# One decoder layer on one core: the end reads x1 and y ahead of the last two down weights and splits the last sum between DVE and PE; the start fills two experts' operands early

## The chip, the cores and the metric

The kernel runs on one core of a Trainium2 chip. The number that counts is the device time of one execution in microseconds (us). The engines are PE (matrix multiply), DVE (vector), ACT (scalar), POOL (GpSimd) and SP, which here only issues transfers; every engine works through its own instructions in the order in which they are written. ACT and POOL issue some transfers too. The transfers of all three run on the core's 16 DMA engines.

## The reference, cut to what matters

One layer: a mixer (differential attention and latent attention), an output projection, a LayerNorm that gives x1, a router that picks 4 of 32 experts for each of 512 tokens, the experts, and a second LayerNorm.

```python
x = layer_norm(DN_ALPHA * x + mixed, ln1_g[l], ln1_b[l])          # x1
logits = (xt @ w_router + b_router); top_logit, top_idx = lax.top_k(logits, TOP_K)
gates = jax.nn.softmax(top_logit, axis=-1)
# each expert, for the tokens that chose it:
h = xb @ w_gate_up[e] + b_gate_up[e]
act = (up + 1.0) * (gate * jax.nn.sigmoid(gate * SWIGLU_ALPHA))   # gate and up are clamped halves of h
y = act @ w_down[e] + b_down[e]                                    # weighted by the token's gate and summed
x = layer_norm(DN_ALPHA * x + y, ln2_g[l], ln2_b[l])
```

All is float32. The experts' weights are 32 x (8 MB gate and up + 4 MB down); each is read once, in pieces of 1 MB.

## The kernel before

**Tiles.** The 512 tokens are four tiles of 128. Attention goes through (tile, head) units in an order written out by hand (`ORDER`, `PLAN`); after each tile come its output projection, LayerNorm, router logits, and `ranks`, which counts the tile's tokens for each expert. The last two tiles go through `last_two`.

**Weight stream.** `Stream` holds a list of pieces in the order of use: w_in, w_o, then for expert b its 8 gate-and-up pieces, with the 4 down pieces of expert b-1 behind them; the last are gate-and-up of expert 31, down of 30, down of 31. `ahead()` (the issue is L165) sends the next pieces on SP while there are free 1 MB rooms (`raw`, 11 in the ring and a twelfth later) and while `hold` and `limit` allow. SP works in order, so a transfer that waits holds up all that stand behind it. Here "piece" means such a 1 MB read.

**Experts.** For b = 0 to 31: `gu(b)` (gate and up, 8 steps, one piece each, with small tasks of `between(k)` ahead of each step), `swiglu(b)`, and then `down(b - 1)` (4 pieces). Experts 0 and 1 here are the two least used ones after two tiles (`pick_first`), and have 32 token slots each; 30 and 31 have 64. A gather by POOL brings an expert's token rows from x1 in DRAM (`x1d`) into `xg`; PE transposes them into the operand xT. A scatter by POOL writes the result to `yd` in DRAM. Experts 30 and 31 are kept on the chip instead (`y_keep`) and added by matmuls (`tail_kept`); their scatters only serve a later loop that does not run for these inputs.

**Start of the experts.** At the end of the second `ranks` the kernel picks experts 0 and 1, sends the first weight pieces, and for expert 0 alone computes slot columns (`columns`, `prep_tile`), indices (`prep2`, a small matmul at L1356) and the gather (L1378). `last_two` adds the rows of the last two tiles to expert 0's operand by matmuls with a one-hot matrix (`first_col`, `first_more`, L1346, in the PSUM tile `xT0`). The biases are read on ACT's queue (`bias_early`, L1283) ahead of the last tile's norm. Expert 1's operand is prepared inside `gu(0)` with a gather of its own.

**End.** z holds x1 of the four tiles, ys the four expert rows of each token: eight 1 MB reads of `yd`, two for a tile. z is read by `tail_setup` in `gu(30)` (L1664). In `gu(31)` the first six reads of `yd` (L1726) go out when the stream has nothing more to send but down of 31; `tail_gb` and `tail_gates` (L1678 and others) are small tasks between the steps. After `gu(31)`: `tail_sum` of tiles 0 to 2 on DVE (L1731, four instructions of 128x1024 for a tile), `down(30)`, `tail_add` (identity matmul of z into PSUM at L1749, the kept expert 30 at L1739, then the last two reads of `yd` and tile 3's sum on DVE), `down(31)`, and `tail`: expert 31 added, statistics of each tile (L1775 on DVE, square root on POOL), and `finish`: for tiles 0 to 2 ACT normalises, DVE multiplies (L1788), POOL adds (L1789); tile 3 is all DVE; SP writes out (L1795).

## Time and profile before

| | us |
|---|---|
| three runs | 1361.19, 1361.88, 1357.73 (median 1361.19) |
| the profiled execution | 1357.27 |
| its span, first to last instruction | 1355.4 |
| PE, DVE, ACT, POOL busy | 1239.3, 708.5, 534.1, 154.7 |

The page cuts the span into 40 slices and gives for each the busy share of every engine, the granted TensorE clock and the rate of the transfers. The timeline lists an engine's instructions in order of time, equal neighbours merged, and in brackets how long the engine had been idle before and what released it. The windows give busy time, clock and transfer rate of any stretch.

### The profile page before, as it was taken

Reading aid. Unit: us, or ns where it says so; the run is one execution under the profiler, and the core shown is the slowest. Engines: PE = TensorE matmul, PEld = TensorE weight load, DVE = VectorE, ACT = ScalarE, POOL = GpSimd, SP = SyncE. Lnnn points to the kernel's source line nnn. Section 1 sums busy time; section 2 is a strip of 40 time slices with the busy share of each in tenths; the row PEclk is TensorE's granted clock in tenths of the full one; section 3 lists DMA queues with packets and bytes.
Section 4 is the critical chain, followed back from the end, with each engine's and each line's share of the span. In section 5 each row is a group of like instructions: output and inputs, shape, how many; then the busy total and the mean of one; then the engine's idle time right before and its main releaser. Section 6 shows DMA issues by size and latency. Waiting matters only on the chain.

```text
span 1355.4 us, 17704 instructions
## 1 busy us (share of the span) xinstructions
PE 1239.3 (91%) x6376; PEld 784.1 (58%) x6376; DVE 708.5 (52%) x1279; ACT 534.1 (39%) x795; POOL 154.7 (11%) x177
## 2 busy tenths in 40 slices
PE   6989698787999999899999999998999998999892
PEld 5768597773368853354444675464657754765330
DVE  4554655455279931433533685264657745753055
ACT  3442543311167730323413564254455534643111
POOL 2232200010100001001100100000111000000004
PEclk9999799797999999999999999999999999999797
DMA  9201620469999999999999999999999999999981
GB/s 327 98 1 62 231 100 32 177 225 409 416 419 420 418 420 420 420 415 419 419 372 419 419 418 419 419 420 419 419 418 418 417 417 409 415 419 415 395 363 73
DMA packets 76411, 465.28 MB, mean 343 GB/s; under 512 B 10176, under 2 KB 11376, under 8 KB 26144
## 3 DMA queue, kind: packets, MB, share of 16 engines
q1 hardware_dynamic: 65680, 434.89, 78.5%
q0 software_dynamic: 7584, 18.47, 3.7%
q10 hardware_dynamic: 3056, 10.75, 2.1%
q8 instruction: 52, 0.85, 0.3%
q14 instruction: 39, 0.32, 0.1%
HBM read 445.33 MB, written 25.30 MB: 347 GB/s over the span
## 4 chain that ended last, share of the span: by engine, by line
PE 52%; DMA 31%; DVE 7%; ACT 3%; POOL 2%; issue 1%; ACTq 0%; SPq 0%; POOLq 0%; DVEq 0%
DMA raw<-in_w_gate_up_dram 19%; PE acc L1450 13%; DMA raw<-in_w_down_dram 8%; PE acc L266 8%; PE acc L267 8%; PE acc L268 8%; DVE wlo L260 2%; DMA yr<-yd 1%; DMA raw<-yd 1%; PE ip L266 1%; PE ip L268 1%; PE ip L267 1%; PE po L689 1%; PE zp L268 1%; PE zp L266 1%
## 5 line engine op out<-in xcount | busy, mean ns | idle before, releaser
L260 DVE TENSOR_TENSOR wlo<-raw,whi 128x1024 fp32r<-128x1024 f32 (+3 forms) x331 | 393.7, 1238 | 108.8 <-ACT whi L259 105.6
L259 ACT CAST whi<-raw 128x1024 fp32r<-128x1024 f32 (+3 forms) x331 | 335.1, 1063 | 139.7 <-DMA raw<-in_w_gate_up_dram 48.3
L1450 PE MATMUL acc<-raw,xTs 128*64 128x512 f32 (+1 forms) x1344 | 286.4, 621 | 11.5 <-DMA raw<-in_w_gate_up_dram 10.1
L266 PE MATMUL acc<-whi,xTh 128*128 128x512 f32 x416 | 167.8, 403 | 1.8 <-ACT whi L259 1.6
L267 PE MATMUL acc<-wlo,xTh 128*128 128x512 f32 x416 | 164.0, 394 | 3.1 <-DVE wlo L260 3.0
L1450 PEld LDWEIGHTS acc<-raw,xTs 128*64 128x64 f32 (+1 forms) x1344 | 75.7, 133 | 154.9 <-issue 126.9
L268 PE MATMUL acc<-whi,xTl 128*128 128x512 f32 x416 | 163.7, 393 | 0.0
L1450 PE MATMUL acc<-raw,aTs 128*64 128x512 f32 (+1 forms) x736 | 122.6, 526 | 1.9 <-DMA raw<-in_w_down_dram 1.9
L1561 POOL DMA_INDIRECT yd<-y,idx x34 | 46.1, 1356 | 651.7 <-ACT y L1550 472.2
L1500 DVE TENSOR_SCALAR u<-acc 128x512 f32<-128x512 f32 (+1 forms) x47 | 31.1, 661 | 166.1 <-ACT s L1499 166.1
L266 PEld LDWEIGHTS acc<-whi,xTh 128*128 128x128 f32 x416 | 78.2, 188 | 32.8 <-ACT whi L259 8.9
L1499 ACT ACTIVATE s<-acc 128x512 f32<-128x512 f32 (+1 forms) x47 | 26.9, 573 | 166.0 <-PE acc L1455 91.4
L267 PEld LDWEIGHTS acc<-wlo,xTh 128*128 128x128 f32 x416 | 78.1, 188 | 22.4 <-DVE wlo L260 6.2
L268 PEld LDWEIGHTS acc<-whi,xTl 128*128 128x128 f32 x416 | 78.2, 188 | 17.5
L267 PE MATMUL acc<-wlo,aTh 128*128 128x512 f32 x208 | 81.9, 394 | 4.3 <-DVE wlo L260 4.3
L1450 PEld LDWEIGHTS acc<-raw,aTs 128*64 128x64 f32 (+1 forms) x736 | 41.2, 129 | 73.5 <-issue 61.4
L266 PE MATMUL acc<-whi,aTh 128*128 128x512 f32 x208 | 82.4, 396 | 0.5 <-ACT whi L259 0.5
L268 PE MATMUL acc<-whi,aTl 128*128 128x512 f32 x208 | 81.8, 393 | 0.0
L1378 POOL DMA_INDIRECT xg<-x1d,idx x34 | 41.0, 1205 | 307.9 <-issue 168.6
L1550 ACT COPY y<-acc 128x512 f32<-128x512 f32 (+2 forms) x32 | 23.2, 725 | 120.8 <-PE acc L268 72.5
L1358 DVE TENSOR_REDUCE lv<-tp 128x2 f32<-128x4 f32 x35 | 5.6, 159 | 113.6 <-PE tp L1356 113.5
L1406 DVE SCALAR_TENSOR_TENSOR aTl<-tp,aTh 128x512 fp32r<-128x512 f32 x26 | 16.7, 685 | 81.7 <-ACT aTh L1402 81.6
(343 smaller groups left out, 1557.8 us busy)
## 6 DMA issues: line engine op xcount, KB each, us to landing
raw<-in_w_gate_up_dram SPq DMA_DIRECT2D x256, 1024.0 KB, 20.4
raw<-in_w_down_dram SPq DMA_DIRECT2D x128, 1024.0 KB, 21.0
yd<-xg ACTq DMA_DIRECT2D x4, 2048.0 KB
raw<-in_w_in_dram SPq DMA_DIRECT2D x6, 1024.0 KB, 13.7
raw<-yd SPq DMA_DIRECT2D x5, 1024.0 KB, 19.9
raw<-in_w_o_dram SPq DMA_DIRECT2D x4, 1024.0 KB, 5.0
yr<-yd SPq DMA_DIRECT2D x3, 1024.0 KB, 19.9
raw<-in_x_dram SPq DMA_DIRECT2D x4, 512.0 KB, 8.9
```

The source lines that it names most:

```text
L259: nc.scalar.copy(hi[:, js], t[:, js])
L260: nc.vector.tensor_tensor(lo[:, js], t[:, js], hi[:, js].bitcast(F32), op=ALU.subtract)
L266: nc.tensor.matmul(out, l[0], r[0], start=start, stop=False)
L267: nc.tensor.matmul(out, l[0], r[1], start=False, stop=False)
L268: nc.tensor.matmul(out, l[1], r[0], start=False, stop=stop)
L1378: nc.gpsimd.indirect_dma_start(out=B["xg"], out_offset=None, in_=self.rows(self.x1d, n), in_offset=bass.IndirectOffsetOnAxis(ap=B["idx"][: ...
L1406: nc.vector.scalar_tensor_tensor(lo, v, scale, hi.bitcast(F32), op0=ALU.mult, op1=ALU.subtract)
L1450: self.nc.tensor.matmul(o[n * i:n * i + n], lT, r, start=start, stop=stop)
L1499: nc.scalar.activation(s, ps[:, :w], AF.Silu, scale=SW)
L1500: nc.vector.tensor_scalar(u, ps[:, w:2 * w], LIM + 1.0, 1.0 - LIM, op0=ALU.min, op1=ALU.max)
L1550: nc.scalar.copy(y, B["d"])
L1561: self.nc.gpsimd.indirect_dma_start(out=self.rows(self.yd, n), out_offset=bass.IndirectOffsetOnAxis(ap=B["idx"][:, 1:2], axis=0), in_=y, i ...
```

## The change

At the end, x1 of all tiles and the six reads of `yd` for tiles 0 to 2 are issued together at the start of `gu(31)`, behind its last gate-and-up piece and ahead of the down pieces of experts 30 and 31 (`hold` now stops the stream 8 pieces before its end). z is no longer scaled by ACT; gates divided by ALPHA are used in the sums (`ga`) and ALPHA comes in through a diagonal matrix (`diag`). `tail_sum` of tiles 0 to 2 moves into `tail_add`. Tile 3 is split by columns: its second half is summed by PE, with `diag` holding one gate per token (L1830), its first half by DVE, after the statistics of tiles 0 to 2. The scatter of expert 31 moves behind those statistics.

At the start, experts 0 and 1 are both prepared from the first two tiles, in the next two steps of the plan after the second `ranks`; `first_more` adds the last two tiles' rows to both in one matmul of 2 x 32 columns; both operands go to free columns of `xg[0]`. Expert 1's late gather and transposes in `gu(0)` go away, and its slot columns for the scatter move to steps 6 and 7 and into `gu(1)`. The bias reads go to POOL's queue behind the last tile's logits. Five 512-column matmuls whose result nobody reads (`warm`) are added behind the last tile's logits and ranks.

```diff
-            def first_col(q):
-                B = self.blk[0, 0]
-                nc.vector.scalar_tensor_tensor(self.scr[:, :E], self.rk1[:, q], 1.0, self.at0, ...
+            def first_cols(q):
+                mf = w.tile([P, 2, 32], F32, name="mf1", tag="e", bufs=10)
+                for b in range(2):
...
-                    B = self.blk[0, 0] = {}
-                    self.at0 = self.columns(B, 0, w)
-                    for t in ranked:
-                        self.prep_tile((0, 0), t)
-                    self.prep2((0, 0), ranked)
-                    self.gather((0, 0))
+                    self.one = []
+                    early_cols(0)
+                    soon.extend([0, 1])
...
+            def early_rows(b):
+                self.prep2((b, 0), ranked[:2])
+                self.gather((b, 0))
+                if b == 0:
+                    early_cols(1)
+
+            def warm(n):
+                ps = po.tile([P, 512], F32, name="po", tag="po")
+                for j in range(n):
+                    nc.tensor.matmul(ps, self.ident, lng[:, :512], start=j == 0, stop=j == n - 1)
...
-                self.bias_early(nc.scalar)
...
+                self.bias_early(nc.gpsimd)
                 logits2(q)
+                warm(3)
                 self.rank(q)
...
+                warm(2)
+                mq = first_cols(q)
...
                 convert()
+                if soon:
+                    early_rows(soon.pop(0))
...
         self.z = [r[:, j * D:(j + 1) * D] for r in rooms[1:] for j in range(2)]
-        for t in range(NT):
-            nc.sync.dma_start(self.z[t], self.x1d[t * P:(t + 1) * P])
+        self.st.hold = len(self.st.src) - KD
...
         if k == 0:
-            self.ys, self.limit = [], 0
-        if k == 4:
-            self.limit = self.nslots
+            for t in range(NT):
+                nc.sync.dma_start(self.z[t], self.x1d[t * P:(t + 1) * P])
+            self.ys = []
+            self.tail_y(2 * NT - 2)
+            st.hold = len(st.src)
             st.ahead()
-        if k < 4:
-            self.tail_y(2 * NT - 2)
...
-        if k > 3:
-            nc.scalar.mul(self.z[k - 4], self.z[k - 4], ALPHA)
...
     def tail_add(self):
...
         for t in range(NT - 1):
-            self.tail_first(t)
+            self.tail_sum(t, D)
+            for n in range(2):
+                self.tail_first(t, n)
+        self.tail_first(NT - 1, 1)
         self.tail_y(2 * NT)
         self.scatter(B["y"], B, 2)
-        self.tail_sum(NT - 1)
...
-        self.tail_first(NT - 1)
-        self.tail_kept(NT - 1, b, True)
+        self.tail_kept(q, 1, b, False)
+        for k in range(TOPK):
+            nc.tensor.matmul(self.zp[q][1], self.diag[:, k],
+                             self.ys[2 * q + k // 2][:, k % 2 * D + 512:(k % 2 + 1) * D], start=False,
+                             stop=k == TOPK - 1)
+        for t in range(q):
+            stats(t)
+        self.tail_sum(q, 512)
+        self.tail_first(q, 0)
+        self.tail_kept(q, 0, b, True)
         self.scatter(B["y"], B, 2)
-        stats(0)
-        stats(1)
-        for t in range(NT):
-            if t + 2 < NT:
-                stats(t + 2)
+        finish(0)
+        stats(q)
+        for t in range(1, NT):
             finish(t)
```

How the change moves instructions is seen at three places. First SP's transfers at the end of the stream (`raw` from in_w_down are weight pieces, the first four of expert 30, the next four of 31; `yr` and `raw` from yd are the reads of expert rows). Before:

```order
L165 DMA raw_9458<-in_w_gate_up_dram 128x2048
L1664 DMA yr<-x1d 128x1024 x4
...
L165 DMA raw_9494<-in_w_gate_up_dram 128x2048
...
L165 DMA raw_9514<-in_w_down_dram 128x2048
...
L165 DMA raw_9532<-in_w_down_dram 128x2048
L1726 DMA yr<-yd 128x2048 x3
L1726 DMA raw_9550<-yd 128x2048
...
L165 DMA raw_9606<-in_w_down_dram 128x2048
...
L1726 DMA raw_9721<-yd 128x2048
```

After:

```order
L165 DMA raw_9517<-in_w_gate_up_dram 128x2048
L1726 DMA yr<-x1d 128x1024 x4
L1751 DMA yr<-yd 128x2048 x3
L1751 DMA raw_9562<-yd 128x2048
...
L165 DMA raw_9568<-in_w_down_dram 128x2048
...
L165 DMA raw_9620<-in_w_down_dram 128x2048
...
L165 DMA raw_9641<-in_w_down_dram 128x2048
...
L1751 DMA raw_9754<-yd 128x2048
```

The x1 reads now stand behind the last gate-and-up piece, and six reads of `yd` stand ahead of the down pieces of expert 30 instead of behind them.

Second, PE between `down(30)` and the end (`zp` of the four tiles lies in the PSUM tiles `acc` and `tp`; L1450 and L1469 are the expert matmuls, L1428 and L1447 the transposes of expert 31's activations). Before:

```order
L1428 MATMUL tp<-cst,u 128x128 x4
L1749 MATMUL acc<-yr,cst 128x512 x2
L1739 MATMUL acc<-y,mg 128x512 x2
...
L1455 MATMUL acc<-biasr,selw 128x512
L1450 MATMUL acc<-raw_9606,aTs 64x512 x4
...
L1739 MATMUL tp<-y,mg 128x512 x2
L1749 MATMUL acc<-yr,cst 128x512 x2
L1739 MATMUL acc<-y,mg 128x512 x4
```

After:

```order
L1447 MATMUL tp<-cst,u 128x128 x4
L1766 MATMUL acc<-yr,diag 128x512
L1762 MATMUL acc<-y,mg 128x512
...
L1474 MATMUL acc<-biasr,selw 128x512
L1469 MATMUL acc<-raw_9641,aTs 64x512 x4
...
L1830 MATMUL acc<-raw_9754,diag 128x512 x2
L1830 MATMUL acc<-raw_9756,diag 128x512 x2
L1766 MATMUL acc<-yr,diag 128x512
L1762 MATMUL acc<-y,mg 128x512 x2
```

Between the two down products stand seven half tiles instead of six, and behind the second one four matmuls for half of tile 3's sum are new.

Third, PE at the second `ranks` (L1211 and L1228 end `pick_first`; L1356 and L1375 are `prep2` for the early gathers; `po` and `sc` belong to attention). Before:

```order
L1211 MATMUL tp<-sel,oneb 128x32
L1356 LDWEIGHTS m
L1356 MATMUL tp<-orh,m 128x4
...
L689 MATMUL po<-raw_804,pT 128x128
...
L645 MATMUL sc<-raw_474,raw_480 128x128
```

After:

```order
L1228 MATMUL tp<-sel,oneb 128x32
L689 MATMUL po<-raw_804,pT 128x128
...
L645 MATMUL sc<-raw_474,raw_480 128x128
...
L1375 LDWEIGHTS m
L1375 MATMUL tp<-orh,m 128x4
...
L676 MATMUL tp<-cst,e 128x128 x2
```

The first `prep2` moved behind a step of attention; the second one, for expert 1, comes a step later still.

## Rows read from the trace of the kernel before

**Rows 1.** The page: transfer rate (GB/s) in 40 slices of the span

```profile
GB/s 327 98 1 62 231 100 32 177 225 409 416 419 420 418 420 420 420 415 419 419 372 419 419 418 419 419 420 419 419 418 418 417 417 409 415 419 415 395 363 73
```

**Rows 2.** Windows: stretch, length, busy PE, PEld, DVE, ACT, POOL (count), PEclk, DMA share, GB/s

```profile
250.00:258.00 8.00, 2.06 (x17) 1.89 (x15) 5.81 (x32) 1.73 (x6) 0.41 (x1) 0.70 0.23 72
276.00:288.00 12.00, 11.81 (x79) 10.42 (x77) 5.64 (x10) 2.78 (x5) 1.69 (x2) 1.00 0.01 1
310.00:340.00 30.00, 24.33 (x164) 9.80 (x163) 16.88 (x84) 4.73 (x10) 1.59 (x2) 0.75 1.01 420
```

**Rows 3.** Timeline of SP's issues, the last 120 us

```profile
1250.55 7.79 SPq L1664 DMA_DIRECT2D yr<-x1d  x4
1260.62 8.18 SPq L165 DMA_DIRECT2D raw<-in_w_gate_up_dram  x4
1269.69 4.15 SPq L165 DMA_DIRECT2D raw<-in_w_down_dram  x4
1275.97 5.24 SPq L1726 DMA_DIRECT2D yr<-yd  x3
1290.97 7.80 SPq L165 DMA_DIRECT2D raw<-in_w_down_dram  x4
1300.88 2.83 SPq L1726 DMA_DIRECT2D raw<-yd  x2
```

**Rows 4.** Transfer issues from 1230 us on: KB each, median us to landing

```profile
raw<-in_w_down_dram SPq DMA_DIRECT2D x11, 1024.0 KB, 19.8
```

**Rows 5.** Timeline of PE, from gu(31) to the end

```profile
1270.26 1.15 PE L1678 MATMUL tp<-gb,cst 16*128 16x128 f32 x8
1275.93 3.68 PE L1450 MATMUL acc<-raw,xTs 128*64 128x512 f32 x8 [4.52 <-DMA raw<-in_w_gate_up_dram]
1294.98 7.09 PE L1450 MATMUL acc<-raw,aTs 128*64 128x512 f32 x32
1301.99 0.75 PE L1428 MATMUL tp<-cst,u 128*128 128x128 f32 x4
1312.47 1.98 PE L1749 MATMUL tp<-yr,cst 128*128 128x512 f32 x4 [0.41 <-DVE yr L1731]
1315.45 0.51 PE L1455 MATMUL acc<-biasr,selw 128*128 128x512 f32 x1
1315.88 7.09 PE L1450 MATMUL acc<-raw,aTs 128*64 128x512 f32 x32
1323.65 1.99 PE L1739 MATMUL acc<-y,mg 64*128 64x512 f32 x8 [0.69 <-ACT y L1558]
```

**Rows 6.** Timeline of DVE at the end

```profile
1296.86 7.76 DVE L1731 SCALAR_TENSOR_TENSOR yr<-yr,gates 128x1024 f32<-128x1024 f32 x6
1304.65 7.76 DVE L1731 SCALAR_TENSOR_TENSOR yr<-raw,gates,yr 128x1024 f32<-128x1024 f32 x6
1320.76 5.25 DVE L1731 SCALAR_TENSOR_TENSOR yr<-raw,gates,yr 128x1024 f32<-128x1024 f32 x4 [8.35 <-DMA raw<-yd]
1325.93 1.29 DVE L1775 BATCH_NORM_STATS2 bs<-acc 128x6 f32<-128x512 f32 x2
```

**Rows 7.** Timeline of POOL at the end

```profile
1336.24 0.51 POOL L283 TENSOR_SCALAR rs_t<-mv 128x1 f32<-128x1 f32 x1
1338.03 5.83 POOL L1789 TENSOR_TENSOR yr<-yr 128x512 f32<-128x512 f32 x4
```

**Rows 8.** Windows of PE alone: stretch, length, busy (count), PEclk, DMA share, GB/s

```profile
1274.00:1290.00 16.00, 14.06 (x40) 0.50 1.01 420
1308.00:1311.00 3.00, 3.00 (x6) 0.50 1.03 426
```

**Rows 9.** Timeline at the second ranks and up to the third tile's x1 store, by engine

```profile
256.37 0.35 PE L1356 MATMUL tp<-orh,m 128*128 128x4 bf16 x2 [5.94 <-DVE m L1315]
287.44 0.33 SPq L788 DMA_DIRECT2D x1d<-z  x1
303.92 1.07 ACT L783 COPY x1T<-tp 128x512 f32<-128x512 f32 x2 [9.64 <-DMA braw<-in_b_gate_up_dram]
```

More of the change, by code (lines that the diff above doesn't have):

```diff
@@ L860, in attention @@
             tasks = (mix_all, lambda q: out_proj(q, 0), lambda q: out_proj(q, 1), norm, logits, logits2, ranks)
-            todo, late = [], []
+            todo, late, soon = [], [], []
             def flush():
@@ L922, in attention @@
             assert ended == len(started) and [f for f, _ in todo[:2]] == [logits2, ranks] and len(todo) == 9
+            assert not soon
             last_two(*done[-2:])
@@ L1063, in moe @@
         self.oh = mp.tile([P, 2, E], F32, name="oh")
-        xT = mp.tile([P, 2, 4, 32], F32, name="xTs", tag="xTh")
-        nc.scalar.copy(xT, self.xT0[:, :256].rearrange("p (k h s) -> p k h s", k=2, h=4))
+        for b in range(2):
+            xT = self.xg[0][:, 512 + 256 * b:768 + 256 * b].rearrange("p (k h s) -> p k h s", k=2, h=4)
+            nc.scalar.copy(xT, self.xT0[:, b * 256:(b + 1) * 256].rearrange("p (k h s) -> p k h s", k=2, h=4))
+            self.blk[b, 0]["xT"] = xT
         self.rest()
@@ L1076, in first_between @@
         def first_between(k):
-            if k == 0:
-                self.columns(self.blk.setdefault((1, 0), {}), 1, mp)
-                self.prep((1, 0))
-            elif k == 2:
-                self.prep2((1, 0))
-                self.gather((1, 0))
-            elif k == 3:
+            if k == 2:
                 for b in range(2):
@@ L1153, in moe @@
                     self.load_xT(u)
-            if b == KEPT[1]:
-                for t in range(NT - 1):
-                    self.tail_sum(t)
             if b > 0:
@@ L1334, in prep_sel, with first_rows @@
                 self.nc.vector.tensor_scalar(B["sel"][j], self.oneb, oh[j], None, op0=ALU.mult)
-    def first_rows(self, rows):
-        for k in range(2):
-            self.nc.tensor.matmul(self.xT0[:, k * P:(k + 1) * P], rows[:, k * P:(k + 1) * P], self.ident,
-                                  start=k == 0, stop=False)
+    def first_rows(self):
+        for b in range(2):
+            for k in range(2):
+                c = b * 256 + k * P
+                self.nc.tensor.matmul(self.xT0[:, c:c + P], self.xg[b][:, k * P:(k + 1) * P], self.ident,
+                                      start=c == 0, stop=False)
     def first_more(self, rows, mf, last):
@@ L1345, in first_more @@
             c = k % 2 * P + k // 2 * 32
-            self.nc.tensor.matmul(self.xT0[:, c:c + 32], rows[:, k * P:(k + 1) * P], mf, start=False,
-                                  stop=last and k == KD - 1)
+            o = self.xT0.rearrange("p (b n) -> p b n", b=2)[:, :, c:c + 32]
+            self.nc.tensor.matmul(o, rows[:, k * P:(k + 1) * P], mf, start=False, stop=last and k == KD - 1)
     def prep2(self, u, tiles=range(NT)):
@@ L1726, in tail_y, with tail_sum @@
             self.nc.sync.dma_start(self.ys[-1], yv[t, :, j * 2 * D:(j + 1) * 2 * D])
-    def tail_sum(self, t):
+    def tail_sum(self, t, w):
         for k in range(TOPK):
-            self.nc.vector.scalar_tensor_tensor(self.z[t], self.ys[2 * t + k // 2][:, k % 2 * D:(k % 2 + 1) * D],
-                                                self.gates[:, t, k:k + 1], self.z[t], op0=ALU.mult, op1=ALU.add)
-    def tail_kept(self, t, b, stop):
-        B = self.blk[b, 0]
-        for n, o in enumerate(self.zp[t]):
-            ns = slice(64 * n, 64 * n + 64)
-            self.nc.tensor.matmul(o, B["mg"][ns, t * P:(t + 1) * P], B["y"][ns], start=False, stop=stop)
@@ L1741, in tail_first @@
-    def tail_first(self, t):
-        if t == 2:
-            self.zp[t] = [self.tp() for _ in range(2)]
-        else:
-            v = self.acc()
-            self.zp[t] = [v[:, n * 512:(n + 1) * 512] for n in range(2)]
-        for n, o in enumerate(self.zp[t]):
-            self.nc.tensor.matmul(o, self.ident, self.z[t][:, n * 512:(n + 1) * 512], start=True, stop=False)
-        self.tail_kept(t, KEPT[0], False)
+            self.nc.vector.scalar_tensor_tensor(self.z[t][:, :w], self.ys[2 * t + k // 2][:, k % 2 * D:k % 2 * D + w],
+                                                self.ga[:, t, k:k + 1], self.z[t][:, :w], op0=ALU.mult, op1=ALU.add)
```

59 lines of the change are left out of this document (43 added, 16 removed).

## The prediction

> **What bounds the kernel now.** I read the page's row of transfer rates first [rows 1]: from the tenth slice of the span to the thirty-ninth the transfers run at about 420 GB/s with small dents. One window inside shows what that means: at 310 to 340 us the 16 DMA engines are busy to 1.01 of the time [rows 2] while PE works 24.33 of 30 us. So between the start of the stream and its end PE follows the transfers, and what the change gains or loses there on PE, ACT or DVE is covered. Only two stretches can move the end: what comes before the stream is saturated, and what comes after its bytes run out.
>
> At the start, the transfers stand almost still at 276 to 288 us (1 GB/s, PE busy 11.81 of 12) [rows 2]. SP stands in order behind the store of the third tile's x1, which it issues at 287.44 [rows 9]. This hole ends when PE has brought the third tile that far; the saturated stream begins there.
>
> At the end, the order on SP decides [rows 3]. The last two reads of yd are issued at 1300.88 and 1303.7. A 1 MB read lands 19.8 us after its issue [rows 4], so the second one lands at about 1323.5. DVE waited 8.35 us for the reads, has tile 3's sum at 1320.76 to 1326.0, and goes on with the statistics [rows 6]. PE ends down(31) at 1315.88 + 7.09 = 1322.97 [rows 5], so that two chains arrive nearly together. From there it is epilogue: POOL's four adds end at 1338.03 + 5.83 = 1343.86 [rows 7], 20.9 us behind down(31), and the store and the program's end follow.
>
> All sums below stand on the profiled execution: 1357.27 us, of which its span is 1355.4 and 1.87 lies around it. The median of the three runs is 1361.19, 3.9 above it.
>
> **Tail: the order of the transfers.** The reads of yd go out at 1275.97 for the first and 1300.88 for the seventh, with six reads of yd and four weight pieces issued in between: 24.91 / 10 = 2.49 us for 1 MB [rows 3]. Nothing in this stretch is added or removed, so the last piece of expert 31 should land when it did (last issue 1298.8 + 19.8, about 1318.6). But the change puts six of these megabytes ahead of down of expert 30. Its last piece was issued at 1269.69 + 4.15 = 1273.8; it now goes 6 x 2.49 = 14.9 later and lands at 1273.8 + 14.9 + 19.8 = 1308.5. Before, down(30) was through its last 7.09 us run by 1302.07 [rows 5], and PE used the time up to 1315.45 for the six half tiles of x1 and expert 30.
>
> In the changed kernel PE has to do, from 1308.5 on and in this order: the last quarter of down(30), 7.09 / 4 = 1.8; the four transposes, some 0.6 to the next instruction (0.75 long in the trace); seven half tiles, where one tile (two halves) takes 1312.47 to 1315.45 = 2.98, so 3.5 x 2.98 = 10.4; the bias and down(31), 1315.45 to 1322.97 = 7.5 [rows 5]. That is 20.3 and ends at 1328.8, against 1322.97: **+5.8 us**. All of down(31)'s pieces are there by then, so that PE is the bound and nothing hides this. The y order that the change gives up had the seven halves' work under the landing of down(31).
>
> **Tail: PE's clock.** gu(31) gets its pieces earlier by the 2 MB of x1 (5 us), and ends at about 1285; down of expert 30 begins to land at about 1308.5 - 3 x 2.49 = 1301. PE has nothing for about 16 us. After short pauses PE shows the lower level: at 1308 to 1311 it is busy for 3.00 of 3.00 at clock 0.50 (1.2 GHz), behind a pause for DVE [rows 8]. A quarter of a down product takes 1.8 at full clock, and eight such matmuls 3.68 at half [rows 5], more than the 2.49 between two pieces. If only the first quarter is slow, PE has caught up by the fourth: nothing lost. If the first two are, down(30) ends at 1301 + 2 x 3.68 + 2 x 1.8 = 1311.9 in place of 1310.3: +1.6. I take the middle, **+0.8**. The far end is a row too: at 1274 to 1290 PE was busy 14.06 of 16 us and stayed at 0.50 throughout [rows 8]. By it all four quarters take 3.68, down(30) ends at 1315.7, and the term is +5.4; that is rival B.
>
> The Trainium skill (TensorE: Matmul & The Clock Gate, Part 1: The HAM clock gate) says that "the default state is throttled, and activity releases the throttle". By that rule a restarted PE would soon run at full clock and the term would be near the lower end, 0 to 1.6; the row of 1274 to 1290 differs, since 14.06 busy us released nothing there, and by it the term would be 5.4.
>
> **Tail: behind down(31).** Counted from its end, D. Before: POOL ends at D + 20.9. Now: expert 31's copy and kept tile 0 (the eight L1739 matmuls before take 1.99, two halves some 0.5 to 1, behind a 0.69 wait for ACT) let statistics begin at D + 1.7 [rows 5]. DVE does tiles 0 to 2 first, 1.29 for the pair and some 0.15 between, so 3 x 1.45: D + 6.0. Then the half sum of tile 3, four instructions of half of 5.25 / 4 [rows 6]: 2.7, D + 8.7. PE's diagonal matmul and two kept halves, 1.9 by the four L1749 matmuls in 1.98 [rows 5]: D + 10.6. Statistics of tile 3: D + 12.1. POOL's root to its first add, 1338.03 - 1336.24 = 1.8, and the four adds 5.83 [rows 7], with small steps between: D + 20.1. So **-0.8**. The last read of yd (1323.5) no longer binds, as D is 1328.8 or later. The split itself saves 2.6 on DVE, but the half sum and PE's matmuls now stand in a row behind the statistics, so most of it is given back.
>
> **Tail: at no cost.** Tiles 0 to 2's sums on DVE (15.5 us by the rows of 7.76 for six [rows 6]) follow reads that are issued five megabytes earlier and end around 1303, ahead of 1308.5; if they were late by x, the halves would be late by x minus 5. Building the diagonals lies in the same idle time of DVE. ACT's scalings of z go away off the path. The eight gate tasks of 1.15 on PE [rows 5] keep their place beside the waits for pieces (4.52 for one such piece in the same rows). The x1 reads now wait on SP at a later place for the scatter of expert 29 on POOL; behind them stand y, d30 and d31. With 19.8 us from issue to landing at 2.49 each, seven or eight reads are outstanding, so that a wait of up to some 17 us leaves the transfers busy. Beyond that each microsecond shows.
>
> **Front.** PE waits 5.94 us for `m` ahead of L1356 [rows 9], and at 250 to 258 is busy only 2.06 of 8, clock 0.70 [rows 2]. The change puts attention's po and sc matmuls in front of the first prep2 and so fills a part. Against that, DVE has a second chain of columns (for expert 1, some 2.3 us by the 5.81 busy us that DVE spends here on one expert's chain and the ranks [rows 2]), PE a second prep2 (0.35 [rows 9]) and the 2 x 32 column matmuls. The moved work is some 1.2 us at full clock, and nothing if the clock stays low longer. So the bounds on the start of the saturated stream are -5.94 (all of the wait) and +1; I take -0.6, near the row of what PE has to put in there. One late gather leaves the saturated stretch: -0.3 by its 32 rows of 1024 float32, an eighth of a megabyte, against 2.49 for 1 MB. Together **-0.9**, between -6.2 and +1.
>
> The bias reads go from ACT's queue to POOL's. That removes ACT's wait of 9.64 at 303.92 [rows 9]; who waits for the biases now is the copy that converts them and gu(0)'s bias matmul. On POOL the gathers and tasks of the last tile are queued around them. The five extra matmuls, 0.22 each by 7.09 / 32 and 0.46 by 3.68 / 8 [rows 5], cost 1 to 2.3 us of PE. All this lies behind 288 us where the transfers are busy to 1.01 [rows 2] and PE waits for pieces, so I cost it at nothing; uncovered it would be up to +2.3.
>
> **Sum.** 5.8 + 0.8 - 0.8 - 0.9 = +4.9: 1357.27 + 4.9 = 1362.2 by the profiled execution, 1361.19 + 4.9 = 1366.1 by the median. What a measurement of this kernel can tell from no change is about 0.3%, 4.1 us.
>
> **The rivals.** All times on the median.
>
> A, the forecast: +4.9, with 2.5 to either side by the clock's and the front's bounds: 1363.6 to 1368.6. Some 0.54: slower 0.35, same 0.18, faster 0.01.
>
> B, half clock through down(30): 5.4 in place of 0.8 gives +9.5, 1370.7. For it speaks the row of 1274 to 1290, against it that PE was at full clock for most of 1294 to 1322, where 32 matmuls took 7.09 [rows 5]. Chance 0.13, slower.
>
> C, on the other side: PE is early enough. If it has the halves done by about 1314.4, D is set by the last piece of down(31): 1318.6 + 1.8 = 1320.4, and the end by D + 20.1 = 1340.5 in place of 1343.86, -3.4; with the front's -0.9 this is -4.3, 1356.9. It needs down of expert 30 landed by 1301.6 instead of 1308.5, as it would if the 16 engines served the later pieces beside the reads of yd rather than behind them, or if the x1 and y reads go out much earlier than SP's row suggests. For it: eight reads are outstanding at once, so order of issue need not be order of landing. Against it: 19.8 is the median of all pieces alike [rows 4]. Chance 0.19: faster 0.15, same 0.04.
>
> D, the front gets back the whole wait: -6.2 in place of -0.9, in all -0.4, 1360.8. For it: PE is the engine that ends the hole at 276 to 288. Against it: the wait is for DVE, which gets more to do. Chance 0.14: same 0.12, faster 0.02.
>
> **How the numbers follow.** Faster 0.01 + 0.15 + 0.02 = 0.18; same 0.18 + 0.04 + 0.12 = 0.34; slower 0.35 + 0.13 = 0.48. The predicted time is that of A. The range leaves out half of C below and half of B above, 1356.9 to 1371, widened by a microsecond for the unknown bounds: 1356 to 1372. A alone holds 1363.6 to 1368.6.
>
> **What would show it.** In the changed kernel's SP row the x1 and y reads should follow the last gate-and-up piece, and the last piece of expert 30 be issued near 1288.7 and landed near 1308.5. PE should be idle for some 16 us ahead of down(30) and start it at 0.50. Down(31) should end at 1328.8 or a little later, with no wait ahead of its matmuls; if PE waits there for a piece, C is right. POOL's last add should end 20 us behind it. At the start, the store of the third tile's x1 should be issued near 286.8; at 282 it would be D. The prediction is wrong if the stream's last bytes land earlier or later than about 1323 for another reason than the front, for instance if the x1 reads wait on POOL longer than the outstanding reads cover.

## The result and the profile after

| | before | changed |
|---|---|---|
| median of 8 runs | 1361.95 us | 1369.88 us |
| lowest and highest | 1357.73, 1363.43 | 1364.07, 1371.74 |
| the profiled execution | 1357.27 | 1364.07 |
| its span | 1355.4 | 1362.3 |

The ratio is 1.0064, with a 95% interval of 1.0046 to 1.0083: the change costs 6.3 to 11.3 us, 8.7 in the middle. The forecast was slower, +4.9 us, 1366.1 in a range of 1356 to 1372. The direction and the range hold; the size was too small, and it came as near as it did by luck: two errors had opposite signs.

The two profiled spans differ by 6.9 us. Three places in the tail divide this difference. First SP's issues, to set beside [rows 3] (columns: start, length, queue, line, what is moved, count):

```profile
1255.56 8.05 SPq L1726 DMA_DIRECT2D yr<-x1d  x4
1265.84 5.25 SPq L1751 DMA_DIRECT2D yr<-yd  x3
1273.32 2.86 SPq L1751 DMA_DIRECT2D raw<-yd  x3
1277.18 16.56 SPq L165 DMA_DIRECT2D raw<-in_w_down_dram  x8
1295.86 4.03 SPq L1751 DMA_DIRECT2D raw<-yd  x2
```

The seventh read of yd goes out at 1295.86, before the change at 1300.88. The same reads stand ahead of it in both kernels, so the stream comes **5.0 us earlier**. Then PE, to set beside [rows 5]:

```profile
1295.83 9.42 PE L1469 MATMUL acc<-raw,aTs 128*64 128x512 f32 x32 [17.53 <-DMA raw<-in_w_down_dram]
1305.18 0.74 PE L1447 MATMUL tp<-cst,u 128*128 128x128 f32 x4
1305.76 1.02 PE L1766 MATMUL acc<-yr,diag 128*128 128x512 f32 x2
1306.72 1.12 PE L1762 MATMUL acc<-y,mg 64*128 64x512 f32 x2
...
1320.42 0.49 PE L1474 MATMUL acc<-biasr,selw 128*128 128x512 f32 x1
1320.85 7.09 PE L1469 MATMUL acc<-raw,aTs 128*64 128x512 f32 x32
...
1338.23 1.98 PE L1762 MATMUL acc<-y,mg 64*128 64x512 f32 x4
```

One matmul of the kernel's code in float32 is two instructions in these lines: x1 of one half is "x2", kept expert 30 of one half is "x2". Down(31) ends at 1320.85 + 7.09 = 1327.94, which is 32.1 us behind that seventh read; before the change it ended 22.1 behind it (1322.97). This is **10.0 us later**. PE waits 17.53 us for down of expert 30, needs 9.42 for it, and spends 1305.76 to 1320.42 = 14.66 on the seven halves.

Last DVE and POOL, to set beside [rows 6, 7]:

```profile
1329.79 1.29 DVE L1802 BATCH_NORM_STATS2 bs<-acc 128x6 f32<-128x512 f32 x2 [33.38 <-PE acc L1762]
...
1334.06 3.07 DVE L1756 SCALAR_TENSOR_TENSOR yr<-raw,gk,yr 128x512 f32<-128x512 f32 x4
...
1340.25 1.30 DVE L1802 BATCH_NORM_STATS2 bs<-acc 128x6 f32<-128x512 f32 x2 [1.93 <-PE acc L1762]
```

```profile
1341.89 0.51 POOL L283 TENSOR_SCALAR rs_t<-mv 128x1 f32<-128x1 f32 x1 [1.22 <-DVE mv L956]
...
1344.25 5.82 POOL L1816 TENSOR_TENSOR yr<-yr 128x512 f32<-128x512 f32 x4
```

POOL's last add ends at 1350.07, 22.1 behind down(31) where it was 20.9: **1.2 later**. From there to the end of the span it is 12.2 in place of 11.5: 0.7 later, which the experiments put down to the start and not to the tail. The sum is -5.0 + 10.0 + 1.2 + 0.7 = +6.9. DVE's 33.38 us of idle time ahead of the statistics is the line to remember: whether all of tile 3's sum fits into it depends on when tile 3's reads land, and an experiment below tries it.

At the start, a window to set beside [rows 2] (stretch, length, busy PE, PEld, DVE, ACT, POOL, clock, DMA share, GB/s):

```profile
276.00:288.00 12.00, 11.81 (x84) 10.70 (x83) 8.06 (x18) 3.37 (x6) 1.69 (x2) 1.00 0.28 89
```

The transfers begin again inside this window (89 GB/s instead of 1). And the waits of PE at the early index matmuls, where [rows 9] had 5.94:

```profile
255.40 0.35 PE L1375 MATMUL tp<-orh,m 128*128 128x4 bf16 x2 [3.41 <-DVE m L1332]
259.09 0.34 PE L1375 MATMUL tp<-orh,m 128*128 128x4 bf16 x2 [0.25 <-DVE m L1332]
```

They add up to 3.7 us. The store of the third tile's x1 is issued at 284.12 instead of 287.44.

### The profile page after: what moved, and what is told of

Its sections match the earlier page's. It is cut to its first block, busy times and chain, and to the rows that moved or that the text cites. A ratio compares the mean times of both kernels' runs of the same rounds, so it can differ in the third digit from the quotient of the medians.

```text
span 1362.3 us, 17768 instructions
## 1 busy us (share of the span) xinstructions
PE 1244.9 (91%) x6398; PEld 784.4 (58%) x6398; DVE 708.6 (52%) x1302; ACT 530.0 (39%) x791; POOL 157.9 (12%) x185
## 4 chain that ended last, share of the span: by engine, by line
PE 52%; DMA 33%; DVE 6%; ACT 3%; POOL 2%; issue 1%; ACTq 0%; SPq 0%; DVEq 0%; POOLq 0%
DMA raw<-in_w_gate_up_dram 21%; PE acc L1469 12%; DMA raw<-in_w_down_dram 9%; PE acc L266 8%; PE acc L267 8%; PE acc L268 8%; DVE wlo L260 2%; PE ip L266 1%; PE ip L268 1%; PE ip L267 1%; DMA yr<-x1d 1%; PE zp L268 1%; PE zp L266 1%; PE zp L267 1%; PE po L689 1%
## 5 line engine op out<-in xcount | busy, mean ns | idle before, releaser
L1469 PE MATMUL acc<-raw,xTs 128*64 128x512 f32 (+1 forms) x1216 | 261.3, 600 | 5.2 <-DMA raw<-in_w_gate_up_dram 4.5
L1469 PEld LDWEIGHTS acc<-raw,xTs 128*64 128x64 f32 (+1 forms) x1216 | 71.3, 132 | 137.8 <-issue 119.3
L1469 PE MATMUL acc<-raw,aTs 128*64 128x512 f32 (+1 forms) x736 | 125.7, 536 | 21.4 <-DMA raw<-in_w_down_dram 21.4
L266 PEld LDWEIGHTS acc<-whi,xTh 128*128 128x128 f32 x416 | 79.2, 190 | 35.4 <-ACT whi L259 11.6
L1469 PEld LDWEIGHTS acc<-raw,aTs 128*64 128x64 f32 (+1 forms) x736 | 41.5, 130 | 95.2 <-issue 60.4
## 6 DMA issues: line engine op xcount, KB each, us to landing
raw<-in_w_gate_up_dram SPq DMA_DIRECT2D x256, 1024.0 KB, 20.4
raw<-in_w_down_dram SPq DMA_DIRECT2D x128, 1024.0 KB, 21.1
raw<-yd SPq DMA_DIRECT2D x5, 1024.0 KB, 19.9
```

The lines of the kernel that those rows point to most:

```text
L266: nc.tensor.matmul(out, l[0], r[0], start=start, stop=False)
L1469: self.nc.tensor.matmul(o[n * i:n * i + n], lT, r, start=start, stop=stop)
```

## The experiments

All kernels of this section were timed against the kernel before in five or more rounds; ratios are to it, with 95% intervals. "To D" is the time from the issue of the seventh read of yd to the end of down(31), and "D to POOL" from there to the end of POOL's last add, "to end" from there to the end of the span, all from the profiled execution. "2 to 3" is the time from the store of the second tile's x1 to that of the third, "3 to y" from there to the seventh read of yd.

| | ratio | 2 to 3 | 3 to y | to D | D to POOL | to end |
|---|---|---|---|---|---|---|
| before | 1 | 45.82 | 1013.44 | 22.1 | 20.9 | 11.5 |
| changed | 1.0064 (1.0046 to 1.0083) | 43.47 | 1011.74 | 32.1 | 22.1 | 12.2 |
| front_only | 0.9978 (0.9967 to 0.9989) | 43.43 | 1011.83 | 22.7 | 20.3 | 12.2 |
| tail_only | 1.0076 (1.0060 to 1.0092) | 46.85 | 1014.05 | 32.1 | 22.1 | 11.6 |
| pair | 1.0042 (1.0027 to 1.0058) | 42.91 | 1011.83 | 28.3 | 22.1 | 12.2 |
| d30_first | 1.0108 (1.0089 to 1.0127) | 43.53 | 1011.82 | 37.4 | 22.1 | 12.2 |
| d30_pair | 1.0003 (0.9985 to 1.0021) | 45.55 | 1011.59 | 24.9 | 22.1 | 12.2 |
| pair_fullsum | 0.9998 (0.9985 to 1.0011) | 45.89 | 1011.83 | 26.2 | 19.9 | 12.3 |
| d30_full | 0.9974 (0.9957 to 0.9991) | 43.56 | 1012.29 | 22.8 | 20.4 | 12.3 |
| front_bias_act | 0.9995 (0.9982 to 1.0008) | 45.92 | 1014.82 | 22.1 | 20.9 | 11.6 |
| front_nowarm | 0.9972 (0.9955 to 0.9990) | 40.13 | 1012.16 | 22.1 | 20.9 | 12.2 |
| bias_pool | 1.0003 (0.9989 to 1.0017) | 45.27 | 1012.65 | 22.7 | 20.3 | 12.2 |
| front_rows_now | 1.0015 (1.0000 to 1.0030) | 49.53 | 1012.45 | 21.1 | 21.9 | 12.3 |

The last column falls into two groups: 11.5 to 11.6 where the biases are read on ACT's queue (before, tail_only, front_bias_act), 12.2 to 12.3 in the ten kernels that read them on POOL's, bias_pool among them, which differs from the kernel before in nothing else. So the 0.7 us at the very end belongs to the place of the bias reads. What it is made of stays open: SP is through with its last issue 1.3 us behind POOL's last add in all thirteen.

**The two ends apart.** front_only is the changed kernel with the end of before, tail_only the kernel before with the changed end; the diff of the change shows both.

```diff
 # front_only: all of the change ahead of the experts' loop and in gu(0), gu(1)
 # tail_only:  all of the change in tail_setup, tail_step, tail_sum, tail_kept, tail_first, tail_add, tail
```

> The changed start with the tail of before. Theory (the start brings the stream forward by about 5 us, and the tail loses what the start gains and more): the last two reads of yd are issued near 1296 instead of 1300.9, down(31) ends near 1318 instead of 1323, and the median is 5 us under before, about 1357. Rival (the start gives 1 us as predicted, and the transfers at the end went out earlier only because the tail's reads were put in another order): last reads of yd near 1300, median about 1361.

> The start of before with the changed tail. Theory (the tail alone costs about 12 us, of which the start pays back 5): median near 1374, last reads of yd issued near 1300.9, down(31) ending near 1333. Rival (the tail costs 8 to 9 and the start nothing): median near 1370, and the issue times of the changed kernel.

Medians: 1357.16 and 1372.29 against 1361.5. The start saves 0.22%, 3.0 us, the end costs 0.76%, 10.3 us; together 7.3, inside the interval of the change. In front_only the median is the theory's, but its profile has the seventh read at 1299.20, near the rival's 1300: its second x1 store came at 243.94 instead of 241.62, ahead of every edit, and hides 2.3 us of the gain there. In tail_only the median lies between theory (1374) and rival (1370): the end costs less than 12 and more than 8 to 9. The read comes at 1305.81 instead of the theory's 1300.9; 3.3 of that is a late second store (244.91). PE pauses 17.47 us ahead of down(30), like the changed kernel, and "to D" is the same 32.1, so none of that is due to the start.

**The order of the matmuls of the halves.** The changed kernel does x1 and kept expert 30 for one column half, then for the other; pair does x1 for both and then expert 30 for both, as the kernel before did.

```diff
             self.tail_sum(t, D)
             for n in range(2):
-                self.tail_first(t, n)
+                self.nc.tensor.matmul(self.zp[t][n], self.diag[:, TOPK], self.z[t][:, n * 512:(n + 1) * 512], ...)
+            for n in range(2):
+                self.tail_kept(t, n, KEPT[0], False)
```

> The changed kernel with one thing different: for tiles 0 to 2 the two matmuls of x1 (both column halves) stand together and the two of the kept expert 30 behind them, as before the change, where the changed kernel alternates them. Theory (two 64-row matmuls on different halves of PE's rows run beside each other only when they are neighbours): four kept matmuls take about 1.05 us instead of 2.1, each tile 2.98 instead of 4.22, so the halves end 3.7 us earlier and the median falls from 1369.9 to about 1366. Rival (the halves are slow because of the clock or the diagonal matrix): each tile still takes about 4.2 and the median stays near 1370.

The timeline of PE in pair, one tile and the seventh half:

```profile
1313.18 1.98 PE L1784 MATMUL acc<-yr,diag 128*128 128x512 f32 x4
1315.09 1.13 PE L1762 MATMUL acc<-y,mg 64*128 64x512 f32 x4
...
1319.12 1.12 PE L1766 MATMUL acc<-yr,diag 128*128 128x512 f32 x2
1320.18 1.12 PE L1762 MATMUL acc<-y,mg 64*128 64x512 f32 x2
```

Four instructions of the kept expert, both column halves, take as long (1.13) as the two of one half take when they stand alone (1.12). The two column halves of the kept expert lie in different partitions, 0 to 63 and 64 to 127. Neighbours in different partitions run beside each other; with x1 matmuls between them they did not, and neither do neighbours in the same partitions (four in 1.98, the last line of PE in the changed kernel above). "To D" falls from 32.1 to 28.3, the 3.7 expected, and the median from 1369.9 to 1366.8. The clock was at 1.00 in both (1309 to 1321 in pair, 1305 to 1321 in the changed kernel), and the diagonal matrix is in both, so the rival is out.

**Down of expert 30 ahead of the reads.** d30_first is the changed kernel with the four down pieces of expert 30 sent ahead of x1 and y.

```diff
         if k == 0:
+            st.hold = len(st.src) - KD // 2
+            st.ahead()
             for t in range(NT):
                 nc.sync.dma_start(self.z[t], self.x1d[t * P:(t + 1) * P])
-            self.ys = []
-            self.tail_y(2 * NT - 2)
...
+            self.ys, self.limit = [], 0
+        if k == 4:
...
+            self.limit = self.nslots
             st.hold = len(st.src)
             st.ahead()
+        if k < 4:
+            self.tail_y(2 * NT - 2)
```

> The changed kernel with one thing different: the four down pieces of expert 30 are sent ahead of the reads of x1 and y, not behind them. Theory (the late down(30) keeps PE from starting the halves): down(30) follows gu(31) with a few us of pause instead of 17.5, and the halves then wait only for the last of the sums on DVE, near 1311; seven halves end near 1318 instead of 1320.4, the median is about 3 us lower, 1367. Rival (PE would have waited for the y reads in any case, so that the order among the reads is worth nothing): median near 1370, with the pause moved from ahead of down(30) to ahead of the halves and the same end of down(31).

It became slower than the changed kernel, 1374.03 to 1369.88. Down(30) follows gu(31) at once, and the pause, 10.2 us, moved ahead of the halves, as the rival said. But the end of down(31) is later too, which neither theory had. The timeline of PE:

```profile
1280.18 7.09 PE L1469 MATMUL acc<-raw,aTs 128*64 128x512 f32 x32
...
1298.14 2.08 PE L1772 MATMUL acc<-yr,diag 128*128 128x512 f32 x2 [10.20 <-DVE yr L1762]
1300.14 2.07 PE L1768 MATMUL acc<-y,mg 64*128 64x512 f32 x2
```

Two instructions take 2.07 us where the changed kernel has 1.12, and so through all seven halves. The windows say why. PE in d30_first (stretch, length, busy, clock, DMA share, GB/s):

```profile
1297.00:1301.00 4.00, 2.86 (x3) 0.50 1.01 420
1301.00:1305.00 4.00, 4.00 (x5) 0.50 1.02 422
...
1321.00:1325.00 4.00, 4.00 (x5) 0.50 0.10 35
1325.00:1329.00 4.00, 4.00 (x9) 0.50 0.00 0
1329.00:1333.00 4.00, 4.00 (x20) 0.96 0.00 0
```

and in the changed kernel:

```profile
1297.00:1301.00 4.00, 4.00 (x14) 0.62 1.01 420
1301.00:1305.00 4.00, 3.96 (x20) 1.00 1.02 422
1305.00:1309.00 4.00, 4.00 (x13) 1.00 0.99 403
1309.00:1313.00 4.00, 4.00 (x8) 1.00 0.50 207
```

Both come out of a pause at clock 0.50 (1.2 GHz). In the changed kernel the clock is at 1.00 before down(30) is through, and the halves, in the same alternating order, run there throughout. In d30_first the halves are the first work behind the pause, and PE, busy without a gap from 1298.14 on, stays at 0.50 until the second down product, which begins at 1326.91.

d30_pair puts both edits together: d30_first with the pairs of pair.

> Down of expert 30 ahead of x1 and y as in d30_first, and the matmuls of tiles 0 to 2 in pairs as in pair. Theory (PE at half clock does not come up again while it alternates full-row and 64-row matmuls, but does in pairs): the clock is back at 1.00 after the first or second tile, the halves wait for the sums on DVE and end about 17 us behind the first of them, down(31) ends about 25 us behind the issue of the last-but-one read of yd instead of 37, and the median is near 1362. Rival (once low, the clock stays low whatever the order): the tiles take about 6 us each, down(31) ends 31 us behind that issue and the median is near 1367.

```profile
1300.32 3.78 PE L1790 MATMUL acc<-yr,diag 128*128 128x512 f32 x4 [10.21 <-DVE yr L1762]
1304.04 1.24 PE L1768 MATMUL acc<-y,mg 64*128 64x512 f32 x4
1305.58 1.95 PE L1790 MATMUL acc<-yr,diag 128*128 128x512 f32 x4 [0.30 <-DVE yr L1762]
```

The pause is the same 10.2 us and the first four instructions are slow (3.78), but the second tile runs at the 1.95 of the upper level; "to D" is 24.9 instead of 37.4 and the median 1361.07. So of these two orders one brought the clock up here within a tile and the other did not in 28 us; d30_full below has the order of d30_pair, and there too the four instructions behind the pause are slow (3.69) and the next four are not (1.13). Which property of the order it is, the runs don't say.

**The split of tile 3.** pair_fullsum is pair with one thing more: DVE sums all of tile 3 ahead of the end of down(31), in its idle time; PE's seventh half and the diagonal matmuls of gates go.

```diff
-        self.tail_first(NT - 1, 1)
         self.tail_y(2 * NT)
+        self.tail_sum(NT - 1, D)
...
-        self.tail_kept(q, 1, b, False)
-        for k in range(TOPK):
-            nc.tensor.matmul(self.zp[q][1], self.diag[:, k], ...)
-        for t in range(q):
-            stats(t)
-        self.tail_sum(q, 512)
-        self.tail_first(q, 0)
-        self.tail_kept(q, 0, b, True)
...
+        # x1 of both halves, kept 30 of both, kept 31 of both; then the order of stats and finish of before
```

> The kernel of pair without the split of tile 3: DVE sums all of tile 3 in the time in which it is idle ahead of the end of down(31), and PE has neither the seventh half ahead of down(31) nor the four diagonal matmuls behind it. Theory (the split costs: 2.1 us ahead of down(31), and statistics of tile 3 wait for the half sum and PE): down(31) ends 2 us earlier, POOL's last add 20 us behind it instead of 22, the median 4.4 us under pair, near 1362.4. Rival (the split saves as it was meant to, the full sum on DVE holds up the statistics): POOL's last add 22 or more behind down(31), median at pair's 1366.8 or above.

```profile
1321.93 5.25 DVE L1756 SCALAR_TENSOR_TENSOR yr<-raw,gk,yr 128x1024 f32<-128x1024 f32 x4 [19.33 <-DMA raw<-yd]
1330.15 1.29 DVE L1805 BATCH_NORM_STATS2 bs<-acc 128x6 f32<-128x512 f32 x2 [2.97 <-PE acc L1762]
...
1335.70 1.29 DVE L1805 BATCH_NORM_STATS2 bs<-acc 128x6 f32<-128x512 f32 x2
```

Tile 3's last read binds the sum's start (19.33), and still the whole sum is done 2.97 us before DVE is wanted, and tile 3's statistics start 1335.70 - 1328.29 = 7.4 behind down(31), not 12.3. "To D" falls by 2.1, "D to POOL" by 2.2; the median is 1361.28, against 1366.84 in pair, somewhat more than the 4.4 expected. The split was a loss in this arrangement.

d30_full puts pair, d30_first and pair_fullsum together.

> The edits of d30_pair and pair_fullsum in one kernel: down of expert 30 ahead of x1 and y, matmuls in pairs, tile 3 summed by DVE alone. By the two, down(31) ends 2.2 us earlier than in d30_pair and the end is 2 us nearer to it: median near 1357, level with front_only, so that everything that the changed tail costs is in its order of reads, its alternating matmuls and its split. If the gains overlap (the sums on DVE become the bound before down(31), since its last reads land there), only part of the 4 us comes: 1359.

PE in d30_full:

```profile
1297.37 3.69 PE L1790 MATMUL acc<-yr,diag 128*128 128x512 f32 x4 [10.19 <-DVE yr L1762]
1300.99 1.13 PE L1768 MATMUL acc<-y,mg 64*128 64x512 f32 x4
...
1312.75 7.09 PE L1469 MATMUL acc<-raw,aTs 128*64 128x512 f32 x32
```

Down(31) ends at 1319.84. The median is 1354.95, the ratio 0.9974: it is faster than both kernels of the change, and level with front_only's 0.9978, the intervals overlapping nearly wholly. Its 22.8 and 20.4 at the end are those of front_only (22.7 and 20.3). So the cost of the changed tail lies in these three together: the reads ahead of down of expert 30, the alternating matmuls and the split; mending the first pays only once the second is mended. What d30_full keeps of the changed tail (x1 read at the start of gu(31), ALPHA in the matmul, the sums between the down products) brings nothing that can be seen.

**The parts of the start.** front_bias_act is front_only with the bias reads back on ACT's queue at the old place, bias_pool the kernel before with the bias reads on POOL at the new place.

```diff
                 self.release(*self.in_ring)
+                self.bias_early(nc.scalar)
...
                 logits(q)
-                self.bias_early(nc.gpsimd)
                 logits2(q)
```

> The kernel of front_only with the bias reads back on ACT's queue at their old place. Theory (the stream's 1.7 us from the third x1 store to the last reads of yd come from moving these small packets out of the stretch where PE runs to its first weights): the wait of ACT of some 9 us is back, gu(0) starts some 3 us later, and 1 to 1.5 us of the gain go, median near 1358.4. Rival (the transfers are saturated there anyway and it does not matter when the biases go): median at front_only's 1357.2, within 0.5.

> The kernel before with one thing different: the bias reads go to POOL's queue behind the last tile's logits, as in the changed kernel. Theory (the place of the bias reads is worth most of what the changed start gains, since front_bias_act lost 3.2 us of front_only's 4.3): ACT's 9.6 us wait is gone, the stretch from the third x1 store to the last reads of yd falls from 1013.4 to about 1011.8, and the median is 2 to 3 us under before, near 1359. Rival (the bias reads only cost where two operands are prepared early): stretch and median as before, 1361.6 within 0.7.

front_bias_act loses 2.3 us by the ratios (0.17%; the two intervals just touch), more than the 1 to 1.5 expected, and its stretch "3 to y" is 3.0 longer than front_only's: the theory holds, but not by its way through gu(0), which starts only 1.1 us later behind the third x1 store (24.6 and 23.5). Turned round, front_bias_act has all of the changed start but the place of the biases, and it is 0.7 us faster than before, which can't be told from zero. bias_pool gains nothing that can be told from zero either: its stretch is 0.8 shorter, not the theory's 1.6, and the 0.7 at the end of the program takes that back. The windows of PE (busy, clock, DMA share, GB/s), first front_bias_act, whose stream starts about 4 us later, then front_only:

```profile
304.00:308.00 4.00, 2.84 (x23) 1.00 0.96 214
308.00:312.00 4.00, 4.00 (x22) 1.00 0.67 200
```

```profile
304.00:308.00 4.00, 4.00 (x18) 1.00 1.01 352
308.00:312.00 4.00, 3.46 (x31) 1.00 1.04 376
312.00:316.00 4.00, 4.00 (x40) 1.00 1.04 288
```

With the biases on ACT's queue the rate falls to about 200 GB/s for 8 us here, and in before and tail_only to 247 and 259 in the lowest window; with them on POOL's no such window from the start of the stream to 336 us is under 288. With all three of before, tail_only and front_bias_act, SP's ten issues behind the third x1 store take about 21 us, with the biases on POOL 11 to 12:

```profile
291.81 21.05 SPq L165 DMA_DIRECT2D raw<-in_w_gate_up_dram  x10
```

```profile
287.95 11.09 SPq L165 DMA_DIRECT2D raw<-in_w_gate_up_dram  x10
```

(first front_bias_act, then front_only). Why the small reads of ACT's queue slow SP's large ones, and those of POOL's queue less, stays open. In bias_pool the rate is kept (303 or more), but gu(0) hardly gains by it. ACT's copy of the first operand there:

```profile
313.67 0.37 ACT L1065 COPY xTs<-xT 128x256 f32<-128x256 f32 x1 [11.42 <-DMA braw<-in_b_down_dram]
```

It waits for the bias reads, and gu(0) starts at 314.09, 26.8 us behind the third x1 store, before 27.6; in front_only, where the operands lie in free columns of another tile, the copy waits for PE alone and gu(0) starts at 310.87, 23.5 behind it. So the new place of the biases paid only together with the rest of the changed start. That it is the new place of the operands which it needs is read from this wait and not tested by itself.

front_rows_now does both index computations and gathers of the start right behind the second ranks.

```diff
                     early_cols(0)
-                    soon.extend([0, 1])
+                    early_rows(0)
+                    early_rows(1)
```

> The kernel of front_only with both early index computations and gathers right behind the second ranks, as before the change for the one, instead of one and two steps of attention later. Theory (PE standing in order behind that small matmul is what the later place avoids): PE waits there 6 us and 3 more for the second expert, the third x1 store comes some 3 to 5 us later behind the second one than the 43.4 of front_only, and the median is 2 to 5 us higher, 1359 to 1362. Rival (the place makes no difference, since attention's work is only done earlier and then waits for the clock): median within 0.7 of 1357.2.

```profile
259.22 0.35 PE L1379 MATMUL tp<-orh,m 128*128 128x4 bf16 x2 [5.92 <-DVE m L1336]
261.82 0.35 PE L1379 MATMUL tp<-orh,m 128*128 128x4 bf16 x2 [2.25 <-DVE m L1336]
```

The two waits add up to 8.2 us where the changed kernel and front_only have 3.7. "2 to 3" is 49.5 instead of 43.4, and the median 1363.28, 5.0 us over front_only by the ratios, for 4.5 us more of waiting. Here PE's wait is on the path, nearly one for one.

front_nowarm is front_only without the five extra matmuls.

```diff
-                warm(3)
...
-                warm(2)
```

> The kernel of front_only without the five extra matmuls. Theory (they keep PE at full clock through the last tile's router and operand matmuls, but the transfers set the pace there): 16 matmuls of the operand take 3.6 us instead of 1.9, gu(0) starts 2 to 4 us later, and the median stays within 0.7 of front_only's 1357.2. Rival (a later gu(0) frees its rooms later and the stream loses what gu(0) loses): median near 1360.

The second set of operand matmuls takes 3.67 instead of 1.89 us and PE's clock falls to 0.50 at 308 to 312, but "3 to y" is 1012.2 against 1011.8 and the median 1357.76 against 1357.16. The five matmuls are hidden, as the prediction had it. The expected late gu(0) did not come: it starts 309.73 - 285.79 = 23.9 us behind the third x1 store, in front_only 310.87 - 287.37 = 23.5.

## Why the prediction was right, and where it was not

**The late down(30): right.** The order of the reads and the pause came as worked out: PE's pause is 17.53 for about 16, and the first quarter starts at 1295.83, which with the 5.0 of the start is 1300.85 where 1301 was forecast. Down(31), with no wait ahead of it, took the 7.5 of the sum. Rival C has a slip: for its D of 1320.4 the 7.5 of bias and down(31) ask for the halves by 1312.9, not 1314.4. With the earlier stream that is 1307.9; they were done at 1320.42, 12.5 us late.

**PE's clock: right in kind, and smaller.** PE started at 0.50 and came up inside the first half of down(30), which ended at 1305.25 + 5.0 = 1310.3: the term was 0, not 0.8. Rival B did not occur in this kernel. d30_first shows that it was no empty fear: there PE stayed low for seven halves and ended down(31) 5 us later behind the seventh read.

**The seven halves: the term that failed.** The prediction took 2.98 for a tile and 3.5 tiles, 10.4. It took the price of a tile from a row in which the two kept matmuls stood as neighbours, though in the order of the changed kernel, listed under the change, they alternate with the x1 matmuls. They took 14.66; 4.2 us were missing. pair shows it: with the old order all seven halves take 1310.30 to 1321.23 = 10.9, so that 3.7 of the 4.2 return.

**Behind down(31): the wrong sign.** The forecast was -0.8, measured +1.2. Statistics of tiles 0 to 2 came at 6.1 (6.0 forecast), the half sum at 9.2 (8.7, as four instructions of half width cost 3.07, not 2.7), PE's part at 12.3 (10.6): x1 and two kept halves are six instructions and took 3.0, where the 1.9 came from a row of four; both kept halves there lie in the same partitions and run one after the other (1.98). POOL took 2.4 to its first add, not 1.8. The step that failed is the same as in the term before, a price that holds only where kept matmuls overlap. And pair_fullsum shows that the prediction's own remark, that the last read of yd no longer binds, should have led further: the full sum on DVE was free.

**The start: too small, in a term that was put at nothing.** Forecast -0.9 in bounds of -6.2 to +1; the seventh read of the profile has -5.0, and front_only, with the 0.7 at the program's end in it, -3.0 by the ratio. Three terms make the -5.0: the second x1 store came 1.0 earlier (no edit lies before it, and it comes anywhere from 240.65 to 245.67 in the thirteen profiles, so this is spread), "2 to 3" is shorter by 2.35 and "3 to y" by 1.7. "2 to 3" was sized at 0.6, by PE work that fills the gap; the wait fell from 5.94 to 3.41 + 0.25, and front_rows_now shows that it counts. Yet front_bias_act, with a shorter wait too (3.12 + 1.26), gains only 0.7 by its ratio, which is near the 0.6; more than that is not shown. What the forecast missed is the place of the biases, which it put at nothing because the DMA engines were busy to 1.01 behind 288 us: 2.3 us lie between front_bias_act and front_only, though by bias_pool the place is worth that only together with the rest of the changed start. Costing it at nothing was a misreading of the share. The window of the kernel before in which the biases are read, and its packets by queue (packets, MB, share of the 16 engines; q10 is ACT's, q1 SP's):

```profile
300.00:304.00 4.00, 1.33 (x9) 1.00 1.05 247
```

```profile
q10 hardware_dynamic: 298, 0.46, 58.4%
q1 hardware_dynamic: 80, 0.52, 46.4%
```

The share is 1.05, at a rate of 247 GB/s: more than half of the engines' time went to 298 bias packets of 1.5 KB on average, while the weights got 0.52 MB in 4 us. The rate, not the share, tells whether weights flow, and [rows 2] held only windows that end ahead of that stretch or start behind it. A full share is not the whole story either: in front_bias_act the second slow window has a share of 0.67. Rival D priced the return of PE's whole wait; 2.3 of the 5.94 came back.

The five extra matmuls were hidden, but their price was misread too: in the changed kernel they are ten instructions and take 2.82 + 1.96 = 4.8 us, not 1 to 2.3.

**The spread of the start.** "2 to 3" is 40.1 to 45.9 among the profiled executions with the changed start (front_rows_now aside), so that one pair of traces does not give its gain; the ratios do. The runs of the changed kernel, 1364.07 to 1371.74, have a similar width, its profile is of its fastest run, and the profile of before (1357.27) lies below all eight of before.

The sum of the tail in the profile is 10.0 + 1.2 = 11.2, tail_only's ratio says 10.3; the forecast had 5.8. The start in the profile is -5.0 + 0.7 = -4.3, front_only's ratio says -3.0; the forecast had -0.9. The 5.4 missing in the tail and the 3.4 missing at the start cancelled in good part, which is luck: 4.9 was forecast, the profile has 6.9 and the ratio 8.7.

## What to carry to other kernels

Price a group of matmuls by a row that has the same neighbours: here two matmuls on different halves of the partitions cost one as long as nothing stood between them. Where the transfers set the pace, read the rate beside the busy share: here a share of 1.05 went with 247 GB/s. Before work is moved to another engine to shorten the end, look at how long the first one idles ahead of it and when its operands land: here 5.25 us of sums fitted between the landing of the last read and the end of down(31), and the split was a loss.

## What the runs showed of the hardware

- Matmuls with 64 rows in partitions 0 to 63 and 64 to 127 overlapped only as neighbours: four instructions took 1.13 us in pairs (pair), two took 1.12 between matmuls over all 128 rows, and four in the same partitions 1.98 (both in the changed kernel), all at clock 1.00.
- Behind a pause of 10.2 us PE stayed at clock 0.50 for 28 us of gapless work in one order of the same kind of matmuls (d30_first) and was back at 1.00 within one tile, 5 us, in the other (d30_pair). Begun at 1.00, the first order ran at 1.00 for its 14.7 us (the changed kernel).
- While eight bias reads of 64 or 128 KB went through ACT's queue, the lowest 4 us window of the stream had 200 (front_bias_act, two such windows in a row), 247 (before) and 259 GB/s (tail_only); with them on POOL's queue the lowest in ten kernels was 288 GB/s (front_only).
- With the bias reads on POOL's queue the span ended 12.2 to 12.3 us behind POOL's last add in ten kernels, with them on ACT's 11.5 to 11.6 in three. Why stays open.
